# Hybrid decoder trunk: the running maximum's rows sent through DRAM, the gates on a side track, the memory's statistics earlier

## The chip, the cores and the metric

The kernel runs on one core of one Trainium2 chip. The metric is the time of one execution on the device, in microseconds. The engines carry the names of the profile: PE is TensorE's matmul, PEld its weight load, DVE is VectorE, ACT is ScalarE, POOL is GpSimd, SP is SyncE, which issues the DMAs.

## The reference

One layer for 256 tokens of 2048 channels. A normalised input is multiplied by one wide matrix (w_in), whose columns go to three groups: a gated linear recurrence (LRU), an mLSTM with four heads, and a block attention (MoBA) with six heads; their outputs go through w_out, then follow a cross-attention into 256 normalised memory tokens and a last norm. The change touches the mLSTM's gates, its scores, and the norm of the memory:

```
lf = log_sigmoid(fg_pre + bf)              # per token and head
b = cumsum(lf);  a = ig - b                # running sums of the forget gate
m = max(inter, max over s <= j of d)       # running maximum, the stabiliser
s = (q . k) * exp(d - m)                   # scores, causal
hm = mem * rsqrt(mean(mem * mem) + 1e-6) * g
```

The kernel handles all 256 tokens as one piece: with `av` = ig - cumsum(lf) and `cm` = running maximum of `av` over the tokens, the weight of key s for query j is exp(av[s] - cm[j]) under a causal mask. So each head needs the row -cm (256 numbers) spread over all 128 partitions, and av as a column per key.

## The kernel before

The projections run as a stream of 164 weight chunks through TensorE, group by group (`GROUPS`): lx, u0, u4, lz0, o0, o1, lz2, q0, q2, q4, k0, k2, k4, z0, v0, v1, z1, z2 (all from w_in), out0 to out3 (w_out), ck0, ck2 (keys of the memory), cq0, cq2, cv; a tail with wo0 to wo3 follows. A chunk is loaded by SP (tile `raw`, four buffers), split into a high half by ACT (`wh`, L197) and a low half by DVE (`wl`, L148), six buffers each, and multiplied by three kinds of matmul: high by high, low by high, high by low. Chunks are numbered from 0; o1 is 32 to 39, q0 44 to 47, q2 48 to 51, q4 52 to 55, out3 132 to 139, ck0 140 to 143, ck2 144 to 147. A chunk of o1 is 12 matmuls of 384 columns, one of out3 12 of 512, one of the groups q, k and c 32 matmuls of 512 and 256 columns.

Nothing is scheduled by a tool: the order in which the code issues instructions is the order of each engine's queue. The main loop over chunk i splits chunk i+4 on ACT and DVE, then issues the matmuls of chunk i, then calls `done` when a group is complete, and then `step()`. A step resumes the generator at the head of `queue` and runs it to its next `yield`. So all work between the projections (evacuations, convolutions, heads) is cut into pieces, one per chunk: what a step issues stands on TensorE behind chunk i, and on DVE and ACT behind the split of chunk i+4. `urgent` puts a generator at the head of the queue, `bg` at its end.

Three generators matter here. `ml_gates` (L555) is put at the end of the queue when o0 is complete, behind `ml_conv` and `ml_qkv`. Its first piece makes lf on DVE (`log1p`, L361, a chain of small instructions on 128x8 numbers, with an exponential on ACT), then the mask and a selection matrix on POOL. After two empty steps its second piece transposes lf and if on TensorE (L586, L587) into `ps`, and DVE makes cumulative sum, av, running maximum and -cm from it (L589 to L592), and splits -cm into two fp32r halves (`nrow`). The third piece transposes av and the normaliser back to columns (L600, L601). `ml_heads` (L644) then computes, per head, the row -cm on all partitions by two matmuls of the selection matrix with the halves (L654), the scores (L663, L664), the weights and the values. `mem_stats` (L1025) loads the memory, squares it on ACT and adds the squares up on POOL (L402, L404), waits two empty steps, and runs `stats("m")` (L417): sums over partitions by matmuls with ones (L426), the power on POOL, a diagonal tile `yt` on DVE (L430), and a matmul that spreads it (L433). The tile `yt` also serves as scratch for the squares of `x1_evac` (L852).

Of the kernel before, what the change touches and what calls it, by code (L numbers as in the profile page):

```python
# [12 lines left out]
OP = mybir.AluOpType  # L13
AX = mybir.AxisListType
PSUM = bass.MemoryType.PSUM

T = 256
D = 2048
# [87 lines left out]
def kernel(ctx: ExitStack, tc: tile.TileContext, xT, memT, x, mem, ws, vec_d, lw_d, fg_d, out):  # L106
    nc = tc.nc
# [9 lines left out]
    selp = ctx.enter_context(tc.tile_pool(name="selp", bufs=1))  # L117
    accp = ctx.enter_context(tc.tile_pool(name="accp", bufs=4, space=PSUM))
    psp = ctx.enter_context(tc.tile_pool(name="psp", bufs=4, space=PSUM))
    ctx.enter_context(tc.manual_schedule())  # L120

    RAW_BUFS, SPLIT_AHEAD, WARM = 4, 4, 4
# [430 lines left out]
        yield  # L553

    def ml_gates():  # L555
        iff = M["if"]
        lf, e = small("lf", 8), small("lf_e", 8)
        f = iff[:, :, 4:8]
        e3 = e.rearrange("p (a b) -> p a b", a=2)
        lf3 = lf.rearrange("p (a b) -> p a b", a=2)  # L560
        stt(e3, f, -1.0, f, OP.mult, OP.max)
        S.activation(e, e, AF.Exp, scale=-1.0)
        log1p(lf, e, "lf")
        stt(lf3, f, 0.0, lf3, OP.min, OP.subtract)
        cmask = small("mask", 512)[:, :384]
        M["mask"] = cmask
        G.memset(cmask, 0.0)
        for sl, n in ((slice(0, 256), 256), (slice(256, 384), 128)):
            G.affine_select(cmask[:, sl], cmask[:, sl], pattern=[[1, n]], compare_op=OP.is_ge, fill=-1e30, base=0,
                            channel_multiplier=-1)  # L570
        w = big(6, 4, 256)[:4]
        sel = selp.tile([128, 4, 128], F32R, name="sel")
        ones_r = ones[:, :128]
        M["sel"] = sel
        for h in range(4):
            G.affine_select(sel[:, h, :], ones_r, pattern=[[0, 128]], compare_op=OP.is_equal, fill=0.0,
                            base=-h, channel_multiplier=1)
        nrow = [selp.tile([128, 256], F32R, name=f"nrow{i}") for i in range(2)]
        for r in nrow:
            G.memset(r.bitcast(F32), 0.0)  # L580
        M["nrow"] = nrow
        yield HARD
        yield HARD
        p = ps()
        for t in range(2):
            P.transpose(p[:4, t * 128:t * 128 + 128], lf3[:, t, :], ident)  # L586
            P.transpose(p[:4, 256 + t * 128:256 + t * 128 + 128], iff[:, t, 0:4], ident)  # L587
        cb, av, cm, ncm = (w[:, i, :] for i in range(4))
        V.tensor_tensor_scan(cb, ones[:4, :], p[:4, 0:256], 0.0, op0=OP.mult, op1=OP.add)  # L589
        tt(av, p[:4, 256:512], cb, OP.subtract)  # L590
        V.tensor_tensor_scan(cm, ones[:4, :], av, 0.0, op0=OP.mult, op1=OP.max)
        V.tensor_scalar(ncm, cm, -1.0, None, op0=OP.mult)  # L592
        tt(cb, ncm, cb, OP.subtract)
        nh, nl = (r[:4, :] for r in M["nrow"])
        V.tensor_copy(nh, ncm)
        tt(nl, ncm, nh.bitcast(F32), OP.subtract)
        yield HARD
        p = ps()
        for t in range(2):
            P.transpose(p[:, t * 8:t * 8 + 4], av[:, t * 128:t * 128 + 128], ident[:4, :4])  # L600
            P.transpose(p[:, t * 8 + 4:t * 8 + 8], cb[:, t * 128:t * 128 + 128], ident[:4, :4])  # L601
        p3 = p[:, :16].rearrange("p (a b) -> p a b", a=2)
        acol, enb = small("acol", 2, 4), small("enb", 2, 4)
        V.tensor_copy(acol, p3[:, :, 0:4])
        S.activation(enb, p3[:, :, 4:8], AF.Exp)
        M["acol"], M["enb"] = acol, enb
        yield HARD

    def ml_qkv():
        u, uc = M["u"], M["uc"]  # L610
# [33 lines left out]
    def ml_heads():  # L644
        qT, qh, kT, v = M["q"], M["qh"], M["uc"], M["v"]
        acol, cmask = M["acol"], M["mask"]
        hh = big(3, 2, 768)
        M["h"] = hh
        E, Sp, PT, ND = {}, {}, {}, {}

        def scores(h):
            pn = ps()
            for i in range(2):
                P.matmul(pn[:, :256], M["sel"][:, h, :], M["nrow"][i], start=i == 0, stop=i == 1)  # L654
            e = small(f"mo_l{h % 3}", 384)
            E[h] = e
            stt(e[:, :256], pn[:, :256], acol[:, 0, h:h + 1], cmask[:, :256], OP.add, OP.add)
            stt(e[:, 256:], pn[:, 128:256], acol[:, 1, h:h + 1], cmask[:, 256:], OP.add, OP.add)
            S.activation(e, e, AF.Exp)
            p = ps()  # L660
            f, hf = FULL[h], HALF[h]
            for sl, s0, j0 in ((slice(0, 256), 0, 0), (slice(256, 384), 128, 128)):
                P.matmul(p[:, sl], kT[:, f, s0:s0 + 128], qT[:, h, j0:256], start=True, stop=False)  # L663
                P.matmul(p[:, sl], kT[:, hf, s0:s0 + 128], qh[:, h, j0:256], start=False, stop=True)  # L664
            tt(e, p[:, :384], e, OP.mult)

        def values(h):
            e = E[h]
            for t in range(2):
                if h % 2 == 0:  # L670
                    ND[t] = ps()
                o = ND[t][:, (h % 2) * 193:(h % 2) * 193 + 193]
                P.matmul(o, e[:, t * 128:t * 128 + 128], v[:, 0, h, :], start=True, stop=t == 0)
                if t:
                    P.matmul(o, e[:, 256:384], v[:, 1, h, :], start=False, stop=True)

        def outputs(hp):
            for t in range(2):
                nd = ND[t][:, :386].rearrange("p (a b) -> p a b", a=2)
                rd = small("ml_rd", 2)  # L680
                tt(rd, nd[:, :, 192], M["enb"][:, t, 2 * hp:2 * hp + 2], OP.max)
                stt(rd, nd[:, :, 192], -1.0, rd, OP.mult, OP.max)
                V.reciprocal(rd, rd)
                for hh_ in range(2):
                    h = 2 * hp + hh_
                    sl = slice(h * 192, h * 192 + 192)
                    stt(hh[:, t, sl], nd[:, hh_, 0:192], rd[:, hh_:hh_ + 1], M["o"][:, t, sl], OP.mult, OP.mult)

        for n in range(6):
            if n < 4:  # L690
                scores(n)
            yield
            if 1 <= n <= 4:
                values(n - 1)
            yield
            if n in (2, 4):
                outputs(n // 2 - 1)
            yield
# [295 lines left out]


    queue = deque()

    def bg(*gens):
        queue.extend(gens)
# [6 lines left out]

    def step(n=1):

        while queue and n > 0:
            try:  # L1010
                if next(queue[0]):
                    return
                n -= 1
            except StopIteration:
                queue.popleft()
# [9 lines left out]
    def mem_stats():  # L1025
        for j in range(10):
# [2 lines left out]
            if j >= 2:  # L1029
                square("m", j - 2)  # L1030
            yield
        yield from idle(2)
        yield from stats("m")

    def call(f, *args):
# [4 lines left out]
    def done(name, a):  # L1040
# [8 lines left out]
            urgent(lru_z(a, 0))  # L1049
        elif name == "o0":  # L1050
            urgent(o_evac(a, 0))
            bg(ml_gates())
        elif name == "o1":
            urgent(o_evac(a, 1))
        elif name == "lz2":
# [139 lines left out]
```

## Time and profile before

| | |
|---|---|
| median of three runs | 522.2 us (521.16 to 522.33) |
| profiled execution | 521.88 us, span 520.2 us |
| PE busy | 507.9 us (98%) |
| DVE busy | 338.0 us (65%) |
| ACT busy | 292.8 us (56%) |
| POOL busy | 54.8 us (11%) |
| granted clock of TensorE, mean | 0.996 |

The span runs from the first to the last instruction; the execution's own time holds 1.7 us more around it. Busy time of PE is a sum of overlapping matmuls: a matmul of 384 columns has a duration of 0.33 us and the next starts 0.17 us after it, so pitches (start to start) are what a sum is made of. A wait stands in brackets behind the instruction that waited, with what ended it.

### The profile page before, as it was taken

Reading aid. Unit: us, or ns where it says so; the run is one execution under the profiler, and the core shown is the slowest. Engines: PE = TensorE matmul, PEld = TensorE weight load, DVE = VectorE, ACT = ScalarE, POOL = GpSimd, SP = SyncE. Lnnn points to the kernel's source line nnn. Section 1 sums busy time; section 2 is a strip of 40 time slices with the busy share of each in tenths; the row PEclk is TensorE's granted clock in tenths of the full one; section 3 lists DMA queues with packets and bytes.
Section 4 is the critical chain, followed back from the end, with each engine's and each line's share of the span. In section 5 each row is a group of like instructions: output and inputs, shape, how many; then the busy total and the mean of one; then the engine's idle time right before and its main releaser. Section 6 shows DMA issues by size and latency. Waiting matters only on the chain.

```text
span 520.2 us, 7578 instructions
## 1 busy us (share of the span) xinstructions
PE 507.9 (98%) x2814; PEld 448.8 (86%) x2814; DVE 338.0 (65%) x531; ACT 292.8 (56%) x476; POOL 54.8 (11%) x70
## 2 busy tenths in 40 slices
PE   8999999999999999999999999999999999999993
PEld 6999889998988888889988888888888888888883
DVE  5958848895397656548645466654658749637574
ACT  5775477678544333353545755543649467546353
POOL 2800001000132100002000000000132003000000
PEclk9999999999999999999999999999999999999998
DMA  8995635467446544435843465478575527734704
GB/s 274 360 412 180 187 120 167 139 221 230 160 160 178 186 161 163 151 92 183 271 155 121 137 209 179 164 272 325 188 264 174 194 66 259 237 128 129 234 3 161
DMA packets 31077, 98.74 MB, mean 190 GB/s; under 512 B 3520, under 2 KB 3904, under 8 KB 31040
## 3 DMA queue, kind: packets, MB, share of 16 engines
q1 hardware_dynamic: 30896, 98.25, 56.9%
q8 instruction: 22, 0.36, 0.3%
q14 instruction: 15, 0.12, 0.1%
q10 hardware_dynamic: 144, 0.01, 0.0%
HBM read 96.15 MB, written 2.10 MB: 189 GB/s over the span
## 4 chain that ended last, share of the span: by engine, by line
PE 85%; issue 6%; POOL 3%; DVE 3%; DMA 1%; ACT 1%; SPq 1%; POOLq 0%; ACTq 0%; DVEq 0%
PE acc_out L284 5%; PE acc_out L282 5%; PE acc_out L283 5%; PE acc_q L260 4%; PE acc_k L260 4%; PE acc_z L284 4%; PE acc_z L282 4%; PE acc_z L283 4%; PE acc_cq L260 3%; PE acc_lz L260 3%; PE acc_q L261 2%; PE acc_k L261 2%; PE acc_o L283 2%; PE acc_o L282 2%; PE acc_o L284 2%
## 5 line engine op out<-in xcount | busy, mean ns | idle before, releaser
L148 DVE TENSOR_TENSOR wl<-raw,wh 128x1024 fp32r<-128x1024 f32 (+3 forms) x166 | 199.6, 1212 | 111.7 <-ACT wh L197 109.3
L197 ACT ACTIVATE wh<-raw 128x1024 fp32r<-128x1024 f32 (+2 forms) x162 | 161.8, 1013 | 44.5 <-DMA raw<-ws 14.8
L282 PE MATMUL acc_out<-wh,a_y 128*128 128x512 f32 x128 | 50.8, 397 | 0.0
L284 PE MATMUL acc_out<-wh,a_y 128*128 128x512 f32 x128 | 49.9, 390 | 0.0
L283 PE MATMUL acc_out<-wl,a_y 128*128 128x512 f32 x128 | 49.8, 389 | 0.0
L282 PE MATMUL acc_z<-wh,a_x 128*128 128x512 f32 x96 | 39.6, 412 | 0.0
L284 PE MATMUL acc_z<-wh,a_x 128*128 128x512 f32 x96 | 37.6, 391 | 0.0
L283 PE MATMUL acc_z<-wl,a_x 128*128 128x512 f32 x96 | 37.5, 390 | 0.0
L260 PE MATMUL acc_k<-a_x,wh 128*128 128x512 f32 x96 | 34.4, 401 | 0.0
L260 PE MATMUL acc_q<-a_x,wh 128*128 128x512 f32 x96 | 34.1, 398 | 0.0
L451 POOL TENSOR_TENSOR w<-ev,rrow 128x512 f32<-128x512 f32 x11 | 17.5, 1589 | 153.6 <-DVE ev L148 153.6
L284 PEld LDWEIGHTS acc_out<-wh,a_y 128*128 128x128 f32 x128 | 24.0, 188 | 5.2
L283 PEld LDWEIGHTS acc_out<-wl,a_y 128*128 128x128 f32 x128 | 24.1, 188 | 4.7
L282 PEld LDWEIGHTS acc_out<-wh,a_y 128*128 128x128 f32 x128 | 24.1, 188 | 4.6
L261 PE MATMUL acc_k<-a_x,wl 128*128 128x256 f32 x96 | 26.9, 280 | 0.0
L261 PE MATMUL acc_q<-a_x,wl 128*128 128x256 f32 x96 | 26.8, 280 | 0.0
L402 POOL TENSOR_TENSOR mask<-mask,yt 128x512 f32<-128x512 f32 x7 | 10.3, 1473 | 147.1 <-ACT yt L401 147.1
L260 PE MATMUL acc_lz<-a_x,wh 128*128 128x512 f32 x64 | 23.3, 406 | 0.0
L260 PE MATMUL acc_ck<-a_m,wh 128*128 128x512 f32 x64 | 23.1, 403 | 0.0
L260 PE MATMUL acc_cq<-a_h,wh 128*128 128x512 f32 x64 | 22.7, 399 | 0.0
L283 PE MATMUL acc_o<-wl,a_x 128*128 128x392 f32 (+1 forms) x64 | 21.6, 338 | 0.0
L282 PE MATMUL acc_o<-wh,a_x 128*128 128x392 f32 (+1 forms) x64 | 21.6, 337 | 0.0
(302 smaller groups left out, 1187.4 us busy)
## 6 DMA issues: line engine op xcount, KB each, us to landing
raw<-ws SPq DMA_DIRECT2D x138, 512.0 KB, 4.1
raw<-ws SPq DMA_DIRECT2D x24, 384.0 KB, 3.1
w<-x SPq DMA_DIRECT2D x8, 512.0 KB, 6.5
raw<-ws SPq DMA_DIRECT2D x8, 392.0 KB, 3.1
w<-memT SPq DMA_DIRECT2D x8, 256.0 KB, 6.1
out<-xg SPq DMA_DIRECT2D x8, 256.0 KB, 3.0
w<-xT SPq DMA_DIRECT2D x7, 256.0 KB, 6.7
raw<-ws SPq DMA_DIRECT2D x4, 256.0 KB, 5.0
```

The source lines that it names most:

```text
L148: V.tensor_tensor(out, a, b, op)
L197: S.activation(h[:, :kc * n], r[:, :kc * n], AF.Copy)
L260: P.matmul(a[m], h[:, sl], both, start=first, stop=False, skip_group_check=True)
L261: P.matmul(a[m][:, :256], l[:, sl], xh, start=False, stop=last, skip_group_check=True)
L282: P.matmul(o, xh[:, sl], mh, start=first, stop=False)
L283: P.matmul(o, xh[:, sl], ml, start=False, stop=False)
L284: P.matmul(o, xl[:, sl], mh, start=False, stop=last)
L402: G.tensor_tensor(sq[which], sq[which], q, OP.add)
L451: G.tensor_tensor(dst, e, rb(which), OP.mult)
```

## The change

The row -cm is written to a DRAM tile of 4 x 256 numbers by one DMA and read back by a second one that repeats it on all 128 partitions; the selection matrix, the two halves and the eight matmuls on them are gone, and DVE reads the row from SBUF. `ml_gates` goes to a list `side` instead of the queue; each step resumes all generators of that list first, and then the queue as before. The two empty steps in front of `stats("m")` are left out.

```
--- before.py
+++ after.py
@@ -13,6 +13,7 @@
 OP = mybir.AluOpType
 AX = mybir.AxisListType
 PSUM = bass.MemoryType.PSUM
+DRAM = bass.MemoryType.DRAM
 
 T = 256
 D = 2048
@@ -117,6 +118,7 @@
     selp = ctx.enter_context(tc.tile_pool(name="selp", bufs=1))
     accp = ctx.enter_context(tc.tile_pool(name="accp", bufs=4, space=PSUM))
     psp = ctx.enter_context(tc.tile_pool(name="psp", bufs=4, space=PSUM))
+    drp = ctx.enter_context(tc.tile_pool(name="drp", bufs=1, space=DRAM))
     ctx.enter_context(tc.manual_schedule())
 
     RAW_BUFS, SPLIT_AHEAD, WARM = 4, 4, 4
@@ -553,6 +555,7 @@
         yield
 
     def ml_gates():
+        yield
         iff = M["if"]
         lf, e = small("lf", 8), small("lf_e", 8)
         f = iff[:, :, 4:8]
@@ -569,18 +572,8 @@
             G.affine_select(cmask[:, sl], cmask[:, sl], pattern=[[1, n]], compare_op=OP.is_ge, fill=-1e30, base=0,
                             channel_multiplier=-1)
         w = big(6, 4, 256)[:4]
-        sel = selp.tile([128, 4, 128], F32R, name="sel")
-        ones_r = ones[:, :128]
-        M["sel"] = sel
-        for h in range(4):
-            G.affine_select(sel[:, h, :], ones_r, pattern=[[0, 128]], compare_op=OP.is_equal, fill=0.0,
-                            base=-h, channel_multiplier=1)
-        nrow = [selp.tile([128, 256], F32R, name=f"nrow{i}") for i in range(2)]
-        for r in nrow:
-            G.memset(r.bitcast(F32), 0.0)
-        M["nrow"] = nrow
-        yield HARD
-        yield HARD
+        yield
+        yield
         p = ps()
         for t in range(2):
             P.transpose(p[:4, t * 128:t * 128 + 128], lf3[:, t, :], ident)
@@ -591,10 +584,11 @@
         V.tensor_tensor_scan(cm, ones[:4, :], av, 0.0, op0=OP.mult, op1=OP.max)
         V.tensor_scalar(ncm, cm, -1.0, None, op0=OP.mult)
         tt(cb, ncm, cb, OP.subtract)
-        nh, nl = (r[:4, :] for r in M["nrow"])
-        V.tensor_copy(nh, ncm)
-        tt(nl, ncm, nh.bitcast(F32), OP.subtract)
-        yield HARD
+        yield
+
+        d = drp.tile([4, 256], F32, name="d_nrow")
+        nc.sync.dma_start(d, ncm)
+        yield
         p = ps()
         for t in range(2):
             P.transpose(p[:, t * 8:t * 8 + 4], av[:, t * 128:t * 128 + 128], ident[:4, :4])
@@ -604,7 +598,10 @@
         V.tensor_copy(acol, p3[:, :, 0:4])
         S.activation(enb, p3[:, :, 4:8], AF.Exp)
         M["acol"], M["enb"] = acol, enb
-        yield HARD
+        yield from idle(4)
+        M["nrow"] = selp.tile([128, 4, 256], F32, name="nrow")
+        nc.sync.dma_start(M["nrow"], d[None, :, :].to_broadcast([128, 4, 256]))
+        yield
 
     def ml_qkv():
         u, uc = M["u"], M["uc"]
@@ -649,12 +646,10 @@
         E, Sp, PT, ND = {}, {}, {}, {}
 
         def scores(h):
-            pn = ps()
-            for i in range(2):
-                P.matmul(pn[:, :256], M["sel"][:, h, :], M["nrow"][i], start=i == 0, stop=i == 1)
+            pn = M["nrow"][:, h, :]
             e = small(f"mo_l{h % 3}", 384)
             E[h] = e
-            stt(e[:, :256], pn[:, :256], acol[:, 0, h:h + 1], cmask[:, :256], OP.add, OP.add)
+            stt(e[:, :256], pn, acol[:, 0, h:h + 1], cmask[:, :256], OP.add, OP.add)
             stt(e[:, 256:], pn[:, 128:256], acol[:, 1, h:h + 1], cmask[:, 256:], OP.add, OP.add)
             S.activation(e, e, AF.Exp)
             p = ps()
@@ -994,6 +989,7 @@
 
 
     queue = deque()
+    side = []
 
     def bg(*gens):
         queue.extend(gens)
@@ -1006,6 +1002,9 @@
 
     def step(n=1):
 
+        for g in list(side):
+            if next(g, True):
+                side.remove(g)
         while queue and n > 0:
             try:
                 if next(queue[0]):
@@ -1029,7 +1028,6 @@
             if j >= 2:
                 square("m", j - 2)
             yield
-        yield from idle(2)
         yield from stats("m")
 
     def call(f, *args):
@@ -1049,7 +1047,7 @@
             urgent(lru_z(a, 0))
         elif name == "o0":
             urgent(o_evac(a, 0))
-            bg(ml_gates())
+            side.append(ml_gates())
         elif name == "o1":
             urgent(o_evac(a, 1))
         elif name == "lz2":
```

The changed kernel's line numbers differ: L579 and L580 answer to L586 and L587, L594 and L595 to L600 and L601, L428, L432 and L435 to L426, L430 and L433, L359 to L357, L367 to L365.

Where the instructions stand now. DVE in group o1; `wl37` is the low half of chunk 37, `w8` the mLSTM's convolution, `lf_e` to `lf` the logarithm of the forget gate. In the kernel before, DVE's queue reads there:

```order
L148 TENSOR_TENSOR wl36_1180<-raw36_1095,wh36_1179 128x768
L151 SCALAR_TENSOR_TENSOR w8_1150<-w7_779,vec_87,w8_1150 128x256 x3
L148 TENSOR_TENSOR wl37_1204<-raw37_1114,wh37_1203 128x768
L151 SCALAR_TENSOR_TENSOR w8_1150<-w7_779,vec_87,w8_1150 128x256 x3
L148 TENSOR_TENSOR wl38_1226<-raw38_1136,wh38_1225 128x768
```

Splits and convolution steps take turns there, one of each per chunk. In the changed kernel DVE's queue reads, from the same split of chunk 36 on:

```order
L150 TENSOR_TENSOR wl36_1182<-raw36_1097,wh36_1181 128x768
L153 SCALAR_TENSOR_TENSOR lf_e_1202<-if_1176 128x8
L367 TENSOR_SCALAR lf_q_1206<-lf_e_1202 128x8
L368 RECIPROCAL lf_q_1206<-lf_q_1206 128x8
L150 TENSOR_TENSOR lf_s_1205<-lf_e_1202,lf_q_1206 128x8
L150 TENSOR_TENSOR lf_s2_1207<-lf_s_1205 128x8
L371 TENSOR_SCALAR lf_q_1206<-lf_s2_1207 128x8
L153 SCALAR_TENSOR_TENSOR lf_q_1206<-lf_q_1206,lf_s2_1207 128x8 x6
L153 SCALAR_TENSOR_TENSOR lf_q_1206<-lf_q_1206,lf_s_1205 128x8
L375 TENSOR_SCALAR lf_1201<-lf_q_1206 128x8
L153 SCALAR_TENSOR_TENSOR lf_1201<-if_1176,lf_1201 128x8
L153 SCALAR_TENSOR_TENSOR w8_1152<-w7_781,vec_89,w8_1152 128x256 x3
```

The logarithm's chain, which stood among the splits of group q4 (behind wl52), stands behind wl36 now, and the scans in the same way behind wl38.

TensorE at the boundary of chunks 34 and 35, the third and fourth of o1, in the kernel before:

```order
L283 MATMUL acc_o11_1186<-wl34_1133,a_x2_162 128x384
L284 MATMUL acc_o11_1186<-wh34_1132,a_x2_162 128x384
L282 MATMUL acc_o10_1185<-wh35_1155,a_x3_225 128x384
L283 MATMUL acc_o10_1185<-wl35_1156,a_x3_225 128x384
L284 MATMUL acc_o10_1185<-wh35_1155,a_x3_225 128x384
```

Nothing stands between the two chunks. TensorE at the same boundary in the changed kernel, where `ps7` is the tile that the scans read:

```order
L285 MATMUL acc_o11_1188<-wl34_1135,a_x2_164 128x384
L286 MATMUL acc_o11_1188<-wh34_1134,a_x2_164 128x384
L579 MATMUL ps7_1275<-ident_115,lf_1201 4x128
L580 MATMUL ps7_1275<-ident_115,if_1176 4x128
L579 MATMUL ps7_1275<-ident_115,lf_1201 4x128
L580 MATMUL ps7_1275<-ident_115,if_1176 4x128
L284 MATMUL acc_o10_1187<-wh35_1157,a_x3_227 128x384
L285 MATMUL acc_o10_1187<-wl35_1158,a_x3_227 128x384
```

The four transposes of lf and if have moved from behind chunk 50 (group q2) to this place; the next four, of av and the normaliser, from behind chunk 52 to behind chunk 36.

DVE in group out3; `a_m3` to `a_m6` are the low halves of the normalised memory, which are made one per chunk, `rstd_m` and `yt` the statistics. In the kernel before, DVE's queue reads around them:

```order
L151 SCALAR_TENSOR_TENSOR a_m6_3939<-w9_3707,vec_87,a_m6_3939 128x256 x2
L357 TENSOR_SCALAR rstd_m_3944<-ps58_3945 128x2
L430 TENSOR_SCALAR yt_3950<-ident_113,rstd_m_3944 128x128 x2
L148 TENSOR_TENSOR wl143_3954<-raw143_3852,wh143_3953 128x1024
L151 SCALAR_TENSOR_TENSOR a_m7_3971<-w9_3707,vec_87,a_m7_3971 128x256 x2
```

They stand ahead of wl143 and a_m7. In the changed kernel DVE's queue reads around the same instructions:

```order
L150 TENSOR_TENSOR wl140_3859<-raw140_3745,wh140_3858 128x1024
L153 SCALAR_TENSOR_TENSOR a_m4_3876<-w6_3623,vec_89,a_m4_3876 128x256 x2
L359 TENSOR_SCALAR rstd_m_3881<-ps54_3882 128x2
L432 TENSOR_SCALAR yt_3887<-ident_115,rstd_m_3881 128x128 x2
L150 TENSOR_TENSOR wl141_3891<-raw141_3778,wh141_3890 128x1024
L153 SCALAR_TENSOR_TENSOR a_m5_3908<-w6_3623,vec_89,a_m5_3908 128x256 x2
```

The statistics stand behind a_m4 instead of a_m6; on TensorE the sums moved from behind chunk 138 to behind chunk 136, and the matmul that reads yt from behind chunk 142 to behind chunk 137.

## Rows read from the trace of the kernel before

**Rows 1.** The page, part 1: TensorE, busy time, share of span, instructions
```profile
PE 507.9 (98%) x2814; PEld 448.8 (86%) x2814; DVE 338.0 (65%) x531; ACT 292.8 (56%) x476; POOL 54.8 (11%) x70
```

**Rows 2.** Waits of TensorE: who, for whom, us in total, times, longest
```profile
PE acc_ck L261 <- DVE wl L148: 0.8, 1, 0.8
```

**Rows 3.** Timeline, PE, group o1: start, us, engine, line, operation, out<-in, shapes [idle<-releaser]
```profile
103.66 0.33 PE L282 MATMUL acc_o<-wh,a_x 128*128 128x384 f32 x1
...
107.82 0.33 PE L282 MATMUL acc_o<-wh,a_x 128*128 128x384 f32 x1
```

**Rows 4.** Timeline, DVE, group o1
```profile
102.18 0.96 DVE L148 TENSOR_TENSOR wl<-raw,wh 128x768 fp32r<-128x768 f32 x1 [1.72 <-ACT wh L197]
103.06 1.52 DVE L151 SCALAR_TENSOR_TENSOR w<-w,vec,w 128x256 f32<-128x256 f32 x3
104.50 0.95 DVE L148 TENSOR_TENSOR wl<-raw,wh 128x768 fp32r<-128x768 f32 x1
```

**Rows 5.** Timeline, DVE, gates (group q2)
```profile
145.28 0.35 DVE L151 SCALAR_TENSOR_TENSOR lf_e<-if 128x8 f32<-128x8 f32 x1
...
145.91 0.24 DVE L365 TENSOR_SCALAR lf_q<-lf_e 128x8 f32<-128x8 f32 x1 [0.28 <-ACT lf_e L562]
...
149.04 0.17 DVE L151 SCALAR_TENSOR_TENSOR lf<-if,lf 128x8 f32<-128x8 f32 x1
```

**Rows 6.** Timeline, ACT, gates (group q2)
```profile
143.36 1.28 ACT L562 ACT_TABLE_LOAD   x1
```

**Rows 7.** Timeline, DVE, the same logarithm for the LRU
```profile
46.44 0.17 DVE L365 TENSOR_SCALAR sp_q<-sp_e 128x4 f32<-128x4 f32 x1 [0.27 <-ACT sp_e L381]
...
48.82 0.17 DVE L373 TENSOR_SCALAR sp<-sp_q 128x4 f32<-128x4 f32 x1
```

**Rows 8.** Busy time by stretch: us; PE, PEld, DVE, ACT, POOL; clock, DMA, GB/s
```profile
46.00:49.00 3.00, 3.00 (x28) 3.00 (x27) 2.31 (x16) 2.80 (x5) 0.00 (x0) 1.00 0.59 195
97.40:114.10 16.70, 16.70 (x98) 16.70 (x98) 14.55 (x28) 11.01 (x16) 0.00 (x0) 1.00 0.57 180
145.20:149.20 4.00, 4.00 (x25) 3.55 (x24) 3.28 (x17) 3.05 (x4) 2.17 (x8) 1.00 0.42 131
```

**Rows 9.** Timeline, DVE, the scans of the gates
```profile
151.40 0.67 DVE L589 TENSOR_TENSOR_SCAN w<-ones,ps 4x256 f32<-4x256 f32 x1
...
153.58 0.41 DVE L148 TENSOR_TENSOR w<-w 4x256 f32<-4x256 f32 x1
```

**Rows 10.** Timeline, PE, transposes of the gates
```profile
150.13 0.27 PE L586 MATMUL ps<-ident,lf 128*4 128x128 f32 x1
...
150.48 0.48 PE L260 MATMUL acc_q<-a_x,wh 128*128 128x512 f32 x1
```

**Rows 11.** Timeline, PE, first head's scores
```profile
167.84 0.40 PE L654 MATMUL ps<-nrow,sel 128*128 128x256 f32 x2
168.08 0.59 PE L663 MATMUL ps<-w,w 128*128 128x256 f32 x2
```

**Rows 12.** The page, part 6: issue, KB each, us to landing
```profile
raw<-ws SPq DMA_DIRECT2D x138, 512.0 KB, 4.1
```

**Rows 13.** Timeline, PE, group out3
```profile
402.38 0.39 PE L282 MATMUL acc_out<-wh,a_y 128*128 128x512 f32 x1
...
407.82 0.50 PE L426 MATMUL ps<-ones,mask 128*128 128x1 f32 x4
```

**Rows 14.** Timeline, ACT, group out3
```profile
399.87 0.91 ACT L232 ACTIVATE a_m<-w,vec 128x256 fp32r<-128x256 f32 x2 [0.34 <-PE acc_out L284]
```

**Rows 15.** Timeline, POOL, group out3
```profile
402.75 0.80 POOL L404 TENSOR_TENSOR mask<-mask 128x256 f32<-128x256 f32 x1
```

**Rows 16.** Timeline, DVE, group out3
```profile
404.89 0.87 DVE L151 SCALAR_TENSOR_TENSOR a_m<-w,vec,a_m 128x256 fp32r<-128x256 f32 x2
...
410.51 0.48 DVE L430 TENSOR_SCALAR yt<-ident,rstd_m 128x128 f32<-128x128 f32 x2 [0.82 <-POOL rstd_m L359]
```

**Rows 17.** Timeline, ACT, group ck0
```profile
421.27 0.63 ACT L852 ACTIVATE yt<-w 128x512 f32<-128x512 f32 x1 [9.16 <-PE ps L433]
```

More of the change, by code (lines that the diff above doesn't have):

```diff
@@ L15 @@
 PSUM = bass.MemoryType.PSUM
+DRAM = bass.MemoryType.DRAM
 T = 256
@@ L119 @@
     psp = ctx.enter_context(tc.tile_pool(name="psp", bufs=4, space=PSUM))
+    drp = ctx.enter_context(tc.tile_pool(name="drp", bufs=1, space=DRAM))
     ctx.enter_context(tc.manual_schedule())
@@ L555, in ml_gates @@
     def ml_gates():
+        yield
         iff = M["if"]
@@ L571, in ml_gates @@
         w = big(6, 4, 256)[:4]
[L572 to L583, printed above, removed]
+        yield
+        yield
         p = ps()
@@ L593, in ml_gates @@
         tt(cb, ncm, cb, OP.subtract)
[L594 to L597, printed above, removed]
+        yield
+        d = drp.tile([4, 256], F32, name="d_nrow")
+        nc.sync.dma_start(d, ncm)
+        yield
         p = ps()
@@ L606, in ml_gates @@
         M["acol"], M["enb"] = acol, enb
-        yield HARD
+        yield from idle(4)
+        M["nrow"] = selp.tile([128, 4, 256], F32, name="nrow")
+        nc.sync.dma_start(M["nrow"], d[None, :, :].to_broadcast([128, 4, 256]))
+        yield
     def ml_qkv():
@@ L651, in scores @@
         def scores(h):
-            pn = ps()
-            for i in range(2):
-                P.matmul(pn[:, :256], M["sel"][:, h, :], M["nrow"][i], start=i == 0, stop=i == 1)
+            pn = M["nrow"][:, h, :]
             e = small(f"mo_l{h % 3}", 384)
             E[h] = e
-            stt(e[:, :256], pn[:, :256], acol[:, 0, h:h + 1], cmask[:, :256], OP.add, OP.add)
+            stt(e[:, :256], pn, acol[:, 0, h:h + 1], cmask[:, :256], OP.add, OP.add)
             stt(e[:, 256:], pn[:, 128:256], acol[:, 1, h:h + 1], cmask[:, 256:], OP.add, OP.add)
@@ L996 @@
     queue = deque()
+    side = []
     def bg(*gens):
@@ L1007, in step @@
     def step(n=1):
+        for g in list(side):
+            if next(g, True):
+                side.remove(g)
         while queue and n > 0:
@@ L1031, in mem_stats @@
             yield
-        yield from idle(2)
         yield from stats("m")
@@ L1051, in done @@
             urgent(o_evac(a, 0))
-            bg(ml_gates())
+            side.append(ml_gates())
         elif name == "o1":
```

## Prediction

> **What bounds the kernel now.** I read the shares of the engines first. TensorE is busy for 507.9 of 520.2 us [rows 1], and the list of its waits has, after the first 14 us, one single entry: 0.8 us in ck2 [rows 2]. So TensorE's queue is the clock of this kernel: an instruction taken out of that queue is worth its own pitch, a wait put into it costs its whole length, and as nothing later on makes TensorE wait, nothing later gives such a loss back. The other engines count only by their lead, the time by which a chunk's low half (wl, written by DVE) is ready before TensorE asks for it. So the second thing to read is the timeline of DVE at the places to which the change moves work, and above all in group o1, where the gates now stand. All times below are on the span's clock of the kernel before.
>
> **The gates, moved from q2 and q4 to o1.** The order of the changed kernel puts the four transposes of lf and if (L579, L580) behind o1's third chunk, wh34, in front of wh35. On DVE the arithmetic that makes lf stands behind wl36. So TensorE now asks for lf in front of chunk 35, and DVE starts to make it when it has done chunk 36: DVE is ahead by its lead alone, and the lead is short here.
>
> TensorE reaches that place at 103.66 [rows 3] (the first of the two rows is the first matmul of chunk 35). DVE starts wl36 only at 102.18, as it waited 1.72 us for ACT's wh36, and is free for the next instruction at 103.06 [rows 4]. From the start of lf_e to L365, with the exponential on ACT between, it takes 0.63 (145.28 to 145.91) [rows 5]; ACT's table load before that exponential, 1.28 us [rows 6], can run while DVE still works on wl36. So L365 starts at 103.69. From there to the end of lf there are two rows to go by. The gates themselves took 3.30 (145.91 to 149.04 + 0.17) [rows 5]. The same logarithm, made for the LRU, took 2.55 from L365 to the end of L373 [rows 7], and the gates' last step adds 0.17, so 2.72. GpSimd was busy for 2.17 of 4.0 us in the first case, and idle in the second as in o1 [rows 8]; I take the second. So lf is ready at 103.69 + 2.72 = 106.41 (at most 106.99), and **TensorE waits 2.75 us** (at most 3.33) where it did not wait before.
>
> The second wait follows from the same queue. Behind lf DVE has a convolution step (1.44, 103.06 to 104.50) and wl37 (0.88, 102.18 to 103.06) [rows 4], then the same again with wl38: 2 x 2.32 = 4.64, to 111.05. Then come the two scans and what follows them up to cb, 151.40 to 153.58 + 0.41 = 2.59 [rows 9], to 113.64 (at most 114.22). The second transposes (L594, L595) need them and stand in front of chunk 37, which TensorE reached at 107.82 [rows 3]. So in front of chunk 37 TensorE is late by 113.64 - 107.82 = 5.82 (at most 6.40) in all; the two waits are parts of this and are not added again. The first transposes lie inside this time, and their 0.35 (150.13 to 150.48) [rows 10] falls away at their old place; the second ones cost the same at either place. **Loss: 5.5 us**, at most 6.05. I see nothing that takes it under 5: every piece is a chain on DVE in which each instruction reads what the one ahead wrote.
>
> The convolution steps, wl39 and wl40 then come late too, but TensorE is later: 113.64 plus two chunks of 2.08 (107.82 - 103.66, halved) [rows 3] is 117.8 for chunk 39, and DVE reaches it at 113.64 + 2.32 = 116.0. No third wait.
>
> **The rows by DMA instead of TensorE.** Eight matmuls (L654) leave TensorE's queue; two of them take 0.24 (167.84 to 168.08) [rows 11], so **0.96 us** is gained. The split of the maximum into two halves (two DVE instructions) and four selections and two fills on GpSimd go as well; neither engine makes TensorE wait, so nothing. For them come two DMAs on SP. The first (4 KB) waits for the scans; behind it stands raw44, which has to wait for wl40 anyway, and that is behind the scans on DVE. The second (512 KB) stands behind raw48; a load of that size lands in 4.1 us [rows 12], and the heads read it first ten chunks later. I cost both at nothing; without this cover it would be 4.1 us once. Reading the row from SBUF instead of PSUM is DVE's business, also nothing. One table load more on ACT (1.28) is covered by its lead. The heads come six chunks earlier, into q2 to z0, with the same spacing.
>
> **The memory's statistics, two steps earlier.** The sums (L428) move from in front of chunk 139 to in front of chunk 137, and TensorE gets there at 402.38 [rows 13]. They read what GpSimd finishes at 402.75 + 0.80 = 403.55 [rows 15], and this cannot move up: it follows a square on ACT behind the split of a_m3, for which ACT itself waited for TensorE's last matmul on that buffer [rows 14]. So TensorE waits 1.17 us. One chunk later stands L435, which needs L432. DVE is done with a_m4 at 405.76, then 0.17 for L359 (as the gates' last small step [rows 5]), 0.82 for GpSimd and 0.48 for L432 [rows 16]: 407.23. TensorE gets there at 403.55 + 0.4 + 2.72 (half of 407.82 - 402.38) [rows 13] = 406.67, so it waits 0.5 us more, or nothing if DVE takes L359 earlier. Together **1.7 us lost**, 1.2 to 1.7. On the other side ACT stood 9.16 us at L852, whose buffer L433 was still to read [rows 17]; that held up wh144, wl144, and with them TensorE's one wait of 0.8 in ck2 [rows 2]. With L435 far ahead this goes: **0.8 us gained**.
>
> **Sum.** The profiled execution took 521.88 (span 520.2, 1.7 outside it); 521.88 - 0.96 + 5.5 + 1.7 - 0.8 = **527.3**. With the upper bounds it is 527.9, with the lower one of the statistics 526.8. The median of the three runs is 0.3 over the profiled one.
>
> **Rivals.**
>
> The clock falls in the new wait. No stretch of before shows TensorE standing so long after its start, and its clock is 1.00 in each stretch read [rows 8]. If it fell to half in the first wait, chunks 35 and 36 would take 8.3 instead of 4.16: 106.41 + 0.35 + 8.32 = 115.08 in front of chunk 37, where the scans make it wait until 113.64 anyway. So it would cost 1.4, and 528.7 in all. (The Trainium skill, TensorE: Matmul & The Clock Gate, section "Why this matters for your kernels", warns that an idle gap between bursts of matmuls drops the clock to half; by that rule this rival is the rule and not the exception, and no run here shows it so far.) Against it: the first wait is short, and the second covers most of the price.
>
> The second wait does not come, only the first: 521.88 - 0.96 + 2.75 + 1.7 - 0.8 = 524.6. For this the scans would have to be done by 106.41 + 0.35 + 4.16 = 110.92 instead of 113.64; the two convolution steps that stand ahead of them are in the order, so I see no way.
>
> On the other side: DVE is early enough in o1. If lf is there before 103.66 and the scans before 107.82, both waits vanish and 521.88 - 0.96 + 1.7 - 0.8 = 521.8 is left, no change; without the statistics' waits it would be 520.1. The point from which this decides is 2.75 us on DVE's timeline. In favour: DVE stood 1.72 us ahead of wl36 [rows 4], so it isn't full. Against: even with that gap closed lf would come 1.0 us late, and the scans 4.1.
>
> That the change doesn't do what it says is no rival here: the order of its instructions shows each of the three moves.
>
> **Chances.** The forecast (526.5 to 528.2) 0.72; the clock 0.09, at 528 to 530; only the first wait 0.08; early enough 0.09, of which half at 521.8 and half under 520.3; rest 0.02, over 530. The range from 524.4 to 529.5 holds the forecast, the second and most of the first rival. Runs of this kernel tell about 0.3% (1.6 us) from no change: faster 0.05, same 0.05, slower 0.90.
>
> **What would show it.** In the profile after, TensorE's waits must list ps (L579) on DVE's lf with about 2.8 us, ps (L594) on DVE's w with some 2.7, ps (L428) on GpSimd's mask with 1.2, and the entry of ck2 must be gone; L654's sel matmuls are absent. If L579 waits less than 1 us, my place of DVE in o1 is wrong, and with it the sign. If the matmuls of chunk 35 and 36 show a pitch above 0.17, it is the clock.

## The result and the profile after

The changed kernel takes 526.63 us (median of four runs, 526.0 to 528.23), the kernel before, on the same chip, 521.89 (521.16 to 522.33). The ratio is 1.0101 with a 95% interval of 1.0085 to 1.0116: slower by 4.7 us, 0.7 under the forecast of 527.3. The profiled execution took 526.86 us, its span is 525.1 (520.2 before), and the mean granted clock 0.989 (0.996 before). Part of that difference is not the change's: between 8 and 13 us, where the first loads arrive, the granted clock was 0.66 in this execution and 1.00 in the one before.

TensorE's busy time, from part 1 of the page (before: [rows 1]), and the list of its waits (who waits for whom, us in total, times, longest; before: [rows 2]):

```profile
PE 509.5 (97%) x2806; PEld 450.8 (86%) x2806; DVE 338.6 (64%) x529; ACT 294.0 (56%) x477; POOL 51.9 (10%) x64
```

```profile
PE ps L579 <- DVE lf L153: 2.8, 1, 2.8
PE acc_lx L269 <- ACT wh L190: 1.9, 1, 1.9
...
PE ps L428 <- POOL mask L406: 1.0, 1, 1.0
PE ps L595 <- DVE w L150: 0.5, 1, 0.5
```

Eight matmuls fewer (2806 against 2814), and yet PE is busy for 1.6 us more. Three of the four waits shown are those that the prediction named: lf, the mask and w. The entry of ck2 in [rows 2] is gone, as is L654. But the wait on w is 0.5 and not 2.7 us. The entry on wh belongs to the first microseconds, where the first loads arrive; it differs from execution to execution (chunk 34 starts between 101.2 and 103.9 us in the thirteen traces of this case, at 101.58 in the one before and at 102.39 in this one), so 0.81 us of the span's difference is not the change's. Below, stretches are compared from a chunk's start to another's.

Timeline of TensorE at the two places in o1; of before, [rows 3]:

```profile
107.46 0.27 PE L579 MATMUL ps<-ident,lf 128*4 128x128 f32 x1 [2.83 <-DVE lf L153]
...
107.81 0.65 PE L284 MATMUL acc_o<-wh,a_x 128*128 128x384 f32 x1
108.26 0.52 PE L285 MATMUL acc_o<-wl,a_x 128*128 128x384 f32 x1
108.58 0.52 PE L286 MATMUL acc_o<-wh,a_x 128*128 128x384 f32 x1
...
113.72 0.22 PE L594 MATMUL ps<-ident,w 4*128 4x4 f32 x1
114.48 0.22 PE L595 MATMUL ps<-ident,w 4*128 4x4 f32 x1 [0.54 <-DVE w L150]
...
114.76 0.45 PE L284 MATMUL acc_o<-wh,a_x 128*128 128x384 f32 x1
```

And of DVE, which TensorE waits for; of before, [rows 4, 5 and 9]:

```profile
102.96 0.96 DVE L150 TENSOR_TENSOR wl<-raw,wh 128x768 fp32r<-128x768 f32 x1 [1.72 <-ACT wh L199]
103.84 0.16 DVE L153 SCALAR_TENSOR_TENSOR lf_e<-if 128x8 f32<-128x8 f32 x1
104.48 0.17 DVE L367 TENSOR_SCALAR lf_q<-lf_e 128x8 f32<-128x8 f32 x1 [0.49 <-ACT lf_e L565]
...
107.14 0.17 DVE L153 SCALAR_TENSOR_TENSOR lf<-if,lf 128x8 f32<-128x8 f32 x1
...
111.84 0.67 DVE L582 TENSOR_TENSOR_SCAN w<-ones,ps 4x256 f32<-4x256 f32 x1
...
114.01 0.41 DVE L150 TENSOR_TENSOR w<-w 4x256 f32<-4x256 f32 x1
```

DVE's chain ran as forecast: wl36, the logarithm (2.83 us from L367 to the end of lf; the forecast took 2.72), two convolution steps and two splits, the scans, and the last instruction done at 114.42. In TensorE's rows, though, matmuls start 0.32 us apart behind the wait (108.26 to 108.58), where 0.17 was the rule. The busy time by stretch (start and end, length, busy us of PE, PEld, DVE, ACT and POOL, granted clock, DMA share, GB/s) shows why; the stretches are the wait, chunk 35, chunk 36 with the second wait, and chunk 37:

```profile
104.40:107.20 2.80, 0.23 (x2) 0.00 (x0) 2.27 (x14) 2.80 (x6) 0.00 (x0) 1.00 0.55 187
107.81:111.54 3.73, 3.73 (x15) 3.73 (x13) 3.62 (x7) 1.76 (x3) 0.00 (x0) 0.54 0.25 68
111.54:114.76 3.22, 2.68 (x18) 2.32 (x17) 3.08 (x7) 0.00 (x0) 0.00 (x0) 1.00 0.68 249
114.76:116.95 2.19, 2.19 (x14) 2.19 (x13) 2.12 (x5) 0.00 (x0) 0.00 (x0) 1.00 0.03 7
```

The granted clock was 0.54 in chunk 35, close to the lower of the two levels, and chunk 35 took 3.73 us instead of 2.08. That is the first rival's mechanism. It is also most of why the second wait shrank: of the 2.2 us by which it fell short of the forecast, 1.65 are the longer chunk 35, after which TensorE came to L594 that much later; the rest are small pieces (0.50 us from the end of lf to chunk 35, where 0.35 had been taken, and the transpose L594, 0.22 us, that runs in the time of the wait). Only this execution of the changed kernel has a trace. The other three have a mean granted clock of 0.992 to 0.994, and where it fell in them is not shown.

The statistics in out3 and ck, on TensorE, DVE, POOL and ACT (before: [rows 13 to 17]):

```profile
408.53 0.61 PE L428 MATMUL ps<-ones,mask 128*128 128x1 f32 x4 [1.05 <-POOL mask L406]
...
411.86 0.67 PE L435 MATMUL ps<-yt,ones 128*128 128x256 f32 x2
```

```profile
407.68 0.79 POOL L406 TENSOR_TENSOR mask<-mask 128x256 f32<-128x256 f32 x1
```

```profile
410.27 0.15 DVE L359 TENSOR_SCALAR rstd_m<-ps 128x2 f32<-128x2 f32 x1
411.23 0.48 DVE L432 TENSOR_SCALAR yt<-ident,rstd_m 128x128 f32<-128x128 f32 x2 [0.82 <-POOL rstd_m L361]
```

```profile
420.18 0.63 ACT L847 ACTIVATE yt<-w 128x512 f32<-128x512 f32 x1 [1.21 <-DVE w L150]
```

L428 waits 1.05 us for the mask, as forecast; L435 follows the last matmul of its chunk at once, since yt is done just ahead of it (411.71). ACT's L847 (L852 of before) waits 1.21 instead of 9.16 us.

### The profile page after: what moved, and what is told of

Same layout as the page of the kernel before. It is cut to its first block, busy times and chain, and to the rows that moved or that the text cites. A ratio compares the mean times of both kernels' runs of the same rounds, so it can differ in the third digit from the quotient of the medians.

```text
span 525.1 us, 7556 instructions
## 1 busy us (share of the span) xinstructions
PE 509.5 (97%) x2806; PEld 450.8 (86%) x2806; DVE 338.6 (64%) x529; ACT 294.0 (56%) x477; POOL 51.9 (10%) x64
## 4 chain that ended last, share of the span: by engine, by line
PE 90%; DVE 3%; issue 2%; ACT 2%; DMA 1%; POOL 1%; SPq 0%; ACTq 0%; POOLq 0%; DVEq 0%
PE acc_out L284 5%; PE acc_out L286 5%; PE acc_out L285 5%; PE acc_k L262 4%; PE acc_q L262 4%; PE acc_z L286 4%; PE acc_z L284 4%; PE acc_z L285 4%; PE acc_cq L262 3%; PE acc_ck L262 3%; PE acc_lz L262 3%; PE acc_q L263 2%; PE acc_k L263 2%; PE acc_v L285 2%; PE acc_v L286 2%
```

## Experiments

Theory: TensorE's queue sets the kernel's time, the two waits in o1 are DVE's chain seen from there, and the three parts of the change add up. Rivals: the DMAs carry a good part of the loss; it is a mere distance between producer and consumer; the fallen clock carries it; the parts hide each other's cost. Every kernel was timed beside the kernel before (medians 522.08, 521.92 and 522.3 us in the three sets), and differences are given against that one.

**The statistics alone (a_stats).**

```
# mem_stats of the kernel before
-        yield from idle(2)
         yield from stats("m")
```

> The kernel before, with only the two idle steps ahead of the memory's statistics taken out. By the prediction's sum TensorE loses 1.7 us (1.2 in front of the sums, 0.5 in front of the broadcast) and gains 0.8 in ck2: +0.9 us against the kernel before. The rival is a reading of the changed kernel's trace, in which the chunks from 136 to 148 move by only +0.2 us in all: the broadcast hardly waits and ck gives more back, so +0.2 us. If the gain in ck2 had another cause than this move, the loss would stand alone, +1.2 to +1.7.

Measured: 522.05 us, ratio 0.9995 (0.9987 to 1.0004), so -0.7 to +0.2 us. Two windows of this kernel, chunk 136 (with the wait at L426) and ck2:

```profile
400.17:404.57 4.40, 3.35 (x18) 2.54 (x16) 4.40 (x4) 3.86 (x7) 2.44 (x3) 1.00 0.43 167
...
425.54:436.85 11.31, 11.31 (x67) 9.81 (x65) 8.22 (x18) 7.19 (x19) 1.54 (x1) 1.00 0.73 239
```

Chunk 136, with the sums, takes 4.40 us where it took 2.71 (399.67 to 402.38), and PE stands 1.05 of it. The whole of 136 to 139, into which the matmul on yt (L433) moves from ck0, takes 13.24 instead of 11.33; then ck0 takes 12.13 instead of 12.80 and ck2 11.31 instead of 12.38. The sum is +0.17 us: the reading of the changed kernel's trace holds, the forecast of +0.9 doesn't.

**The gates' place alone (b_side).**

```
# kernel before, plus the list `side` and its loop in step()
     def ml_gates():
+        yield
         ...                      # each yield HARD -> yield, one more ahead of the columns
-            bg(ml_gates())
+            side.append(ml_gates())
```

> The kernel before, with only the gates moved to the side track, at the same steps as in the changed kernel; the row still goes through the eight sel matmuls, and the statistics stand where they stood. By the prediction the whole loss is DVE's distance to TensorE in o1: +5.1 to +5.5 us, with waits in front of chunks 35 and 37. The rival: a good part of it comes from the two new DMAs on SP's queue (the first waits for the scans, raw44 stands behind it), then this kernel loses less than 3 us.

Measured: 527.93 us, 1.0106 (1.0091 to 1.0122), +4.8 to +6.4 us. TensorE's waits:

```profile
PE ps L587 <- DVE lf L151: 3.1, 1, 3.1
...
PE acc_ck L261 <- DVE wl L148: 0.8, 1, 0.8
PE ps L603 <- DVE w L148: 0.5, 1, 0.5
```

Without any new DMA the loss is there in full, at the same two places. From chunk 34 to chunk 76 (the first of v0), a stretch that holds the gates' old and new place, this kernel takes 134.40 us, the one before 129.10: +5.3.

**The broadcast through DRAM alone (c_dma).**

```
# the changed kernel
-            side.append(ml_gates())
+            bg(ml_gates())       # pieces as in the kernel before, the row's DMA behind the columns
+        yield from idle(2)       # back ahead of stats("m")
```

> The changed kernel with the gates back in the queue at their old place and the two idle steps back ahead of the statistics, so that only the broadcast through DRAM is left of the change. By the prediction eight matmuls leave TensorE's queue and nothing else happens: -1.0 us against the kernel before (8 x 0.12). The rival: the 512 KB that it moves are not covered, because they hold up the loads behind them or the first head: +2 to +4 us. A second rival: the matmuls stood in time that TensorE waits for anyway, 0.

Measured: 521.07 us, 0.9983 (0.9969 to 0.9998), -1.6 to -0.1. The stretch from chunk 48 to 76 takes 87.96 instead of 88.87 us: -0.91 for the eight matmuls, and no wait on the row appears. In the changed kernel itself, the row's DMA (L603) is issued at 130.9 and lands after 4.5 us, its first reader starts at 159.3:

```profile
L153 DVE SCALAR_TENSOR_TENSOR mo_l<-nrow,acol,mask x8: 339/410/482, 159.3 to 196.0; 128x256 f32<-128x256 f32 x4, 128x128 f32<-128x128 f32 x4
L603 SPq DMA_DIRECT2D nrow<-d_nrow x1: 426/426/426, 130.9 to 130.9; - x1
...
DMA to landing us min/median/max: 4.5/4.5/4.5
```

**The gates later on the side track (d_late).**

```
     def ml_gates():
-        yield
+        yield from idle(11)
-        yield from idle(4)
+        yield
         M["nrow"] = ...
```

> The changed kernel with one number altered: the gates wait ten steps more on the side track (and the broadcast is asked for one step behind the columns instead of four), so they stand at lz2 and q0, where DVE is 7 to 10 us ahead of TensorE instead of 2 to 3.5. By the prediction's mechanism the waits at both transposes go, and what is left is -1.0 for the matmuls and +0.2 to +0.9 for the statistics: 0 to -0.8 us against the kernel before. If the loss came from the side track itself, from the clock or from the DMAs, it would stay at +3 us or more.

Measured: 521.11 us, 0.9982 (0.9973 to 0.9991), -1.4 to -0.5. Of the four waits shown of the changed kernel, both of the gates are gone from the list; this one stays:

```profile
PE ps L428 <- POOL mask L406: 1.0, 1, 1.0
```

The side track and the DMAs cost nothing that the timing shows: -1.0 is what the matmuls alone bring. The loss is the place. What differs there is DVE's lead, taken from the end of a chunk's wl to the first matmul of that chunk: 6.4 to 10.4 us at chunks 43 to 47 in this run, 2.2 to 3.5 at chunks 35 to 38 in the kernel before. So the results are there before TensorE asks, lf by 2.4 us and the last of the scans by 4.2:

```profile
129.44 0.17 DVE L153 SCALAR_TENSOR_TENSOR lf<-if,lf 128x8 f32<-128x8 f32 x1
...
131.98 0.27 PE L579 MATMUL ps<-ident,lf 128*4 128x128 f32 x1
...
134.80 0.41 DVE L150 TENSOR_TENSOR w<-w 4x256 f32<-4x256 f32 x1
...
139.46 0.22 PE L594 MATMUL ps<-ident,w 4*128 4x4 f32 x1
```

That DVE's chain sets the loss, and not something else at that place, is tried in g_short.

**More distance at the early place (e_apart).**

```
         w = big(6, 4, 256)[:4]
-        yield
-        yield
+        yield from idle(4)
         p = ps()                 # transposes and scans
         ...
         nc.sync.dma_start(d, ncm)
-        yield
+        yield from idle(3)
         p = ps()                 # columns
```

> The changed kernel with two steps more between the logarithm and the first transposes and two more between the scans and the second ones, so that DVE's results are asked for in front of chunks 37 and 41 instead of 35 and 37. If the loss is only a matter of too short a distance between producer and consumer, it goes: -1.0 us against the kernel before, as with the gates late. If it is DVE's lead, the 3.4 us of the logarithm and the 2.6 us of the scans still stand ahead of wl37 to wl41 while the lead in the kernel before is 1.4 to 2.4 there: TensorE then waits for wl37 (about 1.0) and on, 3.7 in all by chunk 41, and +2.5 to +3 us remain against the kernel before.

Measured: 523.39 us, 1.0035 (1.0022 to 1.0048), +1.1 to +2.5. The waits for lf and w are gone, and the splits wait in their place:

```profile
PE acc_lz L263 <- DVE wl L150: 0.6, 1, 0.6
...
PE acc_o L285 <- DVE wl L150: 0.3, 1, 0.3
```

So both readings were half right. Of the loss a part is bare distance, which the longer way takes off; the rest is work for which DVE has no room. By the start of chunk 42 TensorE is 3.3 us later than in the kernel before, counted from chunk 34 (22.93 instead of 19.61), where 3.7 had been expected: it asks for the low half a few matmuls after the chunk's start. What the expectation missed is what comes back: the transposes stand inside these 3.3 us and are gone from their old place, and the stretch from chunk 48 to 76 is 2.1 us shorter (86.75 instead of 88.87), of which it had counted only the 1.0 of the matmuls. 3.3 - 2.1 + 0.2 for the statistics is +1.4.

**The first wait filled (f_fill).**

```
         p = ps()
+        for _ in range(6):
+            P.matmul(p[:, :256], ones[:, :128], ones, start=True, stop=True)
         for t in range(2):
             P.transpose(p[:4, t * 128:t * 128 + 128], lf3[:, t, :], ident)
```

> The changed kernel with six idle matmuls of 128x256 on the constant ones (0.43 us each in the warm-up, 2.6 in all) put in front of the first transposes, so that TensorE has work for most of its 2.8 us of waiting. What they write is overwritten by the transposes. If the waiting makes the clock fall, chunk 35 takes its 2.1 us again instead of 3.7. If the scans set chunk 37, the time does not change: +4.7 us against the kernel before (within 0.5), and the wait in front of the second transposes grows from 0.5 to about 2.2 us. If the fall has a price of its own, the time falls by 1.0 to 1.65 us, to +3.1 to +3.7.

Measured: 527.18 us, 1.0105 (1.0087 to 1.0123), +4.5 to +6.4. The stretches are chunk 35 with full clock, the second wait, and chunks 37 and 38:

```profile
107.69:109.89 2.20, 2.20 (x16) 2.20 (x14) 2.17 (x4) 1.76 (x3) 0.00 (x0) 1.00 0.02 4
...
112.20:114.64 2.44, 0.50 (x5) 0.40 (x5) 2.30 (x6) 0.00 (x0) 0.00 (x0) 1.00 0.66 217
114.64:117.59 2.95, 2.95 (x15) 2.95 (x14) 2.81 (x7) 0.00 (x0) 0.00 (x0) 0.72 0.02 6
117.59:120.52 2.93, 2.93 (x13) 2.93 (x13) 2.16 (x5) 1.23 (x3) 0.00 (x0) 0.69 0.69 203
```

The fill did what it should: chunk 35 takes 2.20 us at clock 1.00, and the second wait grew to 2.0 (0.76 and 1.25 us at its two places). But chunk 37 starts no earlier for it, 12.40 us behind chunk 34, where the changed kernel has 12.37: the clock that stays up in chunk 35 gains nothing. And now the clock falls behind the second wait, to 0.72 and 0.69, and nothing stands behind that to cover it: 2.95 and 2.93 us instead of 2.08, 1.7 lost. So the expectation of an unchanged time (+4.7 within 0.5) was missed by a little in the medians, +5.3, and clearly in the trace (48.11 us from chunk 34 to 48, the changed kernel 46.48).

**A shorter logarithm (g_short).**

```
-        for c in (13, 11, 9, 7, 5, 3):
+        for c in (13, 11, 9, 7, 5, 3)[6 if name == "lf" else 0:]:
             stt(q, q, 1.0 / c, s2, OP.add, OP.mult)
```

> The changed kernel with six of DVE's steps left out of the gates' logarithm (the terms of its series), 1.2 us of the 3.4 from the row of seven such steps (1.37). This leaves out a part of what the logarithm computes. If the chain on DVE sets the loss, the whole 1.2 us come back: +3.5 us against the kernel before, a first wait of 1.6 us instead of 2.8, and the scans done 1.2 us earlier. If the clock sets it, more comes back, up to 2.8 us (the 1.65 of chunk 35 with it). If the place in the order sets it, whatever DVE does there, nothing comes back: +4.7.

Measured: 525.46 us (524.4 to 527.31), 1.0075 (1.0058 to 1.0092), +3.0 to +4.8. The first wait is 1.7 us, and chunk 37 starts 11.20 us behind chunk 34, in the changed kernel 12.37: the 1.2 us come back there, to a tenth. Again the clock holds in chunk 35 and falls in chunks 37 and 38, which together take 5.86 us, in the changed kernel 4.27:

```profile
105.77:107.97 2.20, 2.20 (x15) 2.20 (x13) 2.17 (x4) 2.20 (x5) 0.00 (x0) 1.00 0.02 6
...
112.72:115.64 2.92, 2.92 (x14) 2.92 (x13) 2.79 (x6) 0.00 (x0) 0.00 (x0) 0.73 0.02 6
115.64:118.58 2.94, 2.94 (x13) 2.94 (x13) 2.18 (x4) 1.20 (x3) 0.00 (x0) 0.68 0.64 201
```

So the chain on DVE sets the start of chunk 37, as forecast; what the time makes of it depends on where the clock falls. The profiled execution, with the fall in chunks 37 and 38, took 526.42 us, the fastest run 524.4. Only the profiled one has a trace, so that the fall was missing in the others is likely, not shown.

**Both waits filled (j_fill2).**

```
# f_fill, and ahead of the columns' transposes
+        for _ in range(5):
+            P.matmul(p[:, :256], ones[:, :128], ones, start=True, stop=True)
```

> The changed kernel with both waits filled: six idle matmuls in front of the first transposes and five (2.1 us) in front of the second ones. If the fall of the clock behind the second wait is what the kernel with one fill paid (chunks 37 and 38 took 2.95 and 2.93 us instead of 2.08, 1.7 in all), the clock stays at 1.00 through o1, and the time is that of DVE's chain alone: +4.0 to +4.7 us against the kernel before, below the kernel with one fill. If the clock has no share in the time, it stays at +5.3.

Measured: 526.23 us (525.86 to 526.6), 1.0075 (1.0063 to 1.0087), +3.3 to +4.5. The clock stays at 1.00 through o1; three stretches around the second wait:

```profile
112.40:114.40 2.00, 2.00 (x12) 1.55 (x11) 1.90 (x5) 0.00 (x0) 0.00 (x0) 1.00 0.64 234
114.40:116.40 2.00, 2.00 (x14) 2.00 (x13) 1.93 (x4) 0.00 (x0) 0.00 (x0) 1.00 0.03 8
116.40:118.40 2.00, 2.00 (x13) 2.00 (x12) 1.96 (x3) 0.00 (x0) 0.00 (x0) 1.00 0.62 221
```

From chunk 34 to 48 this kernel takes 46.52 us, the one with one fill 48.11, the changed one 46.48. Up to the start of chunk 37 the three agree (12.40, 12.40 and 12.37 us), so DVE sets that time in each. That is the clean statement on the clock: with no fall at all, this stretch takes as long as with the fall in chunk 35, so that fall was free; and a fall in chunks 37 and 38 costs 1.6. What is left, +3.9, is DVE's chain, with what the matmuls gain taken off.

**The diagonal in a tile of its own (h_tile).**

```
# stats() of the kernel before
-        d = small("yt", 512)[:, :256]...
+        d = small("dg" if which == "m" else "yt", 256 if which == "m" else 512)[:, :256]...
```

> The kernel before, with a tile of its own for the diagonal that the memory's statistics write and the broadcast reads (instead of yt, which the squares use too); the two idle steps stay. It asks whether the 0.8 us in ck2 hangs on the statistics' place. By the prediction ACT stands at L852 for a buffer of PSUM that L433 is still to read, so another tile changes nothing: 0 against the kernel before. The rival: what stands in the way is the tile yt, and with its own the wait in ck2 goes, -0.8 to -1.0 us.

Measured: 519.81 us, 0.9963 (0.9949 to 0.9977), -2.7 to -1.2. The expectation put the buffer into PSUM, which the prediction had not said; [rows 17] names it, L852 writes yt. With the diagonal in a tile of its own ACT no longer stands there for 9.16 us. Its row, and the window of ck2:

```profile
413.25 0.63 ACT L852 ACTIVATE yt<-w 128x512 f32<-128x512 f32 x1 [1.34 <-DVE w L148]
```

```profile
423.44:434.53 11.09, 11.09 (x67) 9.70 (x65) 8.22 (x19) 7.18 (x19) 1.54 (x1) 1.00 0.69 218
```

ck0 takes 12.64 instead of 12.80 us and ck2 11.09 instead of 12.38. This is the gain that the earlier statistics bring, without their loss in out3. Of the 2.1 us some 0.6 are not explained by the wait (below, on the two pitches).

**The two gains together (i_best, k_late_best).** The first is c_dma with the tile of its own, the second d_late with that tile and the two idle steps back.

> The row's broadcast through DRAM with the gates at their old place in the queue, the two idle steps kept ahead of the statistics, and the diagonal in a tile of its own. If the gains of the two edits alone add up, -1.0 and -2.1 us: -3.1 us against the kernel before, 518.8. If the wait in ck2 and the matmuls lie in the same slack, less: -2.1.

> The same, but with the gates on the side track ten steps later than in the changed kernel, so that the heads come six chunks earlier. If neither the heads' place nor the side track matters, it is as fast as the one with the gates in the queue, -3.1 us against the kernel before (within 0.5). If the earlier heads bring or cost something, the two differ by more.

Measured: 519.23 us, 0.9947 (0.9931 to 0.9962), and 519.51 us, 0.9949 (0.9936 to 0.9962): -3.1 and -2.8 us. The gains add up, and the gates' place on the side track makes no difference that the timing shows once DVE has the lead for it. Both are faster than the kernel before and than the changed one.

## Why the prediction held, step by step

**The parts add up.** -1.0 (c_dma), +5.8 (b_side) and 0.0 (a_stats) make +4.8; the changed kernel has +4.7, and the intervals of the three leave about 1 us open. The traces are closer: from chunk 34 to chunk 156 they give -1.07, +5.20 and +0.16 us, together +4.29, and the changed kernel +4.30. No part hides another's cost.

**The gates: place, cause and size right.** The first wait was forecast at 2.75 us and took 2.83. The end of the last instruction in front of the second transposes was forecast 5.82 us behind the time at which TensorE reached chunk 37; it came at 114.42, and with the 0.81 us of the start taken off that is 5.79. The net loss from chunk 34 to 76, with the eight matmuls' 0.9 added back, is 5.0 (133.22 against 129.10, and 0.91), forecast 5.5. Most of the 0.5 between them comes back in q2 to z0, though the prediction had said that nothing later gives a loss back: that stretch (chunks 48 to 76) is 2.12 us shorter. The matmuls make up 0.91 of it and the two sets of transposes 0.85 (chunks 50 and 52 of the kernel before took 3.13 and 3.26 us beside 2.77 for chunk 49). That makes 1.76, and by so much the stretch is shorter in d_late, whose heads stand at the same chunks as the changed kernel's. The other 0.36 lie in chunks 48 to 54: each takes 0.04 to 0.06 us less in the changed kernel than in d_late (the two pitches, last section).

**The second wait: wrong as a single number, since the clock's rival came true.** 0.54 instead of 2.7 us. The step that failed is the one that took chunks 35 and 36 at full clock; "the first wait is short" was no reason against a fall, and 0.09 was a small chance for one that stands in four traces (this one, b_side, f_fill and g_short). That the total held all the same is only in part luck, since the prediction had also said that the second wait covers most of the price. The rival's own working was half right: the clock did fall, in one chunk and not two, and the scans covered it whole, so that the rival's +1.4 did not come. The price was set by what stood behind the gap, 0 in one place and 1.6 us in the other. The Trainium skill (TensorE: Matmul & The Clock Gate, section "Why this matters for your kernels") warns against long idle gaps between bursts of matmuls, since the clock drops behind them; the trace agrees with that, 0.54 behind a gap of 2.83 us.

**The row by DMA: right.** 0.96 forecast, 0.91 in the trace of c_dma, and the row lies in SBUF 24 us before its first reader in the changed kernel (130.9 + 4.5 to 159.3).

**The statistics: the mechanism right, two terms mis-sized.** The wait on the mask was 1.05 us (forecast 1.17). The second wait of 0.5, in front of L435, did not come: DVE reached L359 1.74 us behind the start of the sums (408.53 to 410.27), where 2.21 had been worked out (403.55 to 405.76), and TensorE reached L435 0.2 us later than worked out. And what comes back in ck is more than the one listed wait of 0.8: ck2 is 1.07 us shorter, and ck0 loses a short stall as well (the first two transposes at L858 start 0.36 us apart in the kernel before, 0.20 with the tile of its own). Forecast +0.9, by the trace +0.2, by the timed runs -0.7 to +0.2.

Together the gates' 0.5 and the statistics' 0.7 are 1.2 us that the sum had too much: it forecast +5.4, and the traces give +4.3. The medians say +4.7, so that the number came out within 0.7 of the forecast is partly chance.

## What to carry to other kernels

On an in-order queue a moved step costs the time by which its chain on the slow engine ends behind the reader's turn at the new place: here 5 us where DVE led by 2.2 to 3.5 us, and nothing ten steps later, where it led by 6.4 to 10.4. A wait that is lost in one stage can be given back in another when both hang on one tile: look at which tile the long waiting instruction writes (yt at L852), and give one of the two stages a tile of its own before moving work. A fallen clock cost here only what no later wait covered, and a fill or a shorter wait moved the fall to a worse place.

## What was not expected of the hardware

A wait of 2.83 us was followed by one chunk at a granted clock of 0.54, one of 1.7 us (g_short) by a chunk at 1.00, and in the same run two of 0.8 and 1.3 us with one transpose between them by two chunks at 0.73 and 0.68. With both waits filled (j_fill2) the clock stayed at 1.00.

In ck2, cq0 and cq2 a chunk (16 matmuls here and in the groups q and k, not the 32 named at the top) takes 2.83 us in some executions and 2.77 in others, all at a granted clock of 1.00: ck2 11.31 and 11.09 us, cq0 and cq2 together 22.61 and 22.19. The kernel before (without its wait), the changed one and six others show the first, d_late, f_fill, h_tile and the two fastest kernels the second. f_fill and j_fill2 differ in five matmuls 300 us earlier and fall on different sides. It makes 0.64 us over twelve chunks and is part of what h_tile gained. Both pitches also stand within one execution: the kernel before runs chunk 48 at the shorter and chunk 58 at the longer one.

```profile
141.81:144.58 2.77, 2.77 (x18) 2.44 (x17) 2.08 (x4) 2.75 (x4) 1.59 (x2) 1.00 0.54 176
...
172.21:175.04 2.83, 2.83 (x19) 2.45 (x17) 2.45 (x3) 1.06 (x1) 0.00 (x0) 1.00 0.65 204
```

And the traces of the kernel before, a_stats and h_tile, whose code is the same up to the statistics, agree on every chunk from 34 to 135 to 0.01 us. That speaks for the order of the instructions and against the single execution; what in the order sets the pitch stays open.
